# MLP of a decoder block: the second matrix's columns 1024 to 2047 by seven-product blocks too, the residual in HBM meanwhile, another product order and another scheduler

## The chip, the cores and the metric

One core of a Trainium2 chip runs the kernel. The metric is the device time of one execution in microseconds. The median of three runs before the change is 1217.83 us.

Names used below: PE is TensorE (matmuls; PEld its weight loads), DVE is VectorE, ACT is ScalarE, POOL is GpSimd, SP is SyncE, which only issues DMAs here. SBUF is the on-chip memory of 128 partitions, PSUM the eight banks (128 x 512 floats each) into which PE accumulates, HBM the memory outside the core.

## What is computed

One layer of a decoder block on 256 tokens (and 16 meta tokens) of width 2048: two token mixers in parallel, gated and projected, and then an MLP. The change is in the MLP, with small things ahead of it. Cut to what matters:

```python
def reference(...):
    ...
    h = h + rms_norm(m @ w_o[l], g_post_mix[l])
    u = rms_norm(h, g_pre_mlp[l])                         # 256 x 2048
    f = jnp.square(jax.nn.relu(u @ w_up[l])) @ w_down[l]  # 2048 -> 8192 -> 2048
    h = h + rms_norm(f, g_post_mlp[l])
    return h[:, N_META:]
```

All of it is float32. The kernel feeds its matmuls operands cast to the type fp32r, and splits each in two, `hi` (the cast value, made by an ACT copy) and `lo` (the rest, made by a DVE subtraction), and a product of matrices is the sum of three: hi x hi, hi x lo, lo x hi.

## The kernel before

**Stages.** The input projections, the mixers, the gates and the projection by `w_o` come first. From about 544 us on the MLP runs. Its hidden width of 8192 is cut into eight pieces (`NP = 8`) of 1024 features; a piece has two halves h of 512 features, and the 256 tokens have two halves t of 128.

**Up products.** `U{h}{pr}{c}` is a weight block of `w_up`, 1024 rows by 256 columns (half h, pair pr of 128-feature groups, half c of the 2048 rows). It makes hidden features (rows) by tokens (columns) in the PSUM banks u0 and u1, with `mm2_high` (line 418, 512 columns) and `mm2_low` (line 424, 256 columns). After c = 1 the pair of banks is evacuated: `up_pair` adds the two halves of a bank (ACT copy, line 1175; DVE addition, line 1182), and `relu_squared` scales by the row of 1/rms and takes the relu (DVE, line 1201), squares (ACT, line 1206) and writes the activations and their sums and differences ("forms", lines 1217 to 1252) split in hi and lo. That is called an up pair in the prediction. There are eight U blocks and four up pairs in a piece.

**Down products.** A product of a 512 x 512 block of `w_down` with one form of 128 tokens is 12 matmuls of 512 columns (`down`, line 1275). The 2048 output columns are four blocks n of 512. Columns n = 0, 1 are made with a scheme of seven products instead of eight for a 2 x 2 x 2 block (token half, feature half, column block): P1 to P7, each with a weight form made of B11, B12, B21, B22. Two weight forms are made by a DVE addition (`SUM_FOR`, P5 and P6, line 1104), two by a DMA on POOL's queue that adds a block from HBM to a block in SBUF (`BROUGHT_FOR`, P7 and P4, line 1108, "bring"). Each product goes to bank a or b and from there into its block of `F` by a DVE addition (`give`, line 1297). Columns n = 2, 3 are made plainly: X1 to X4, each a weight block used for both token halves, two products each, which stay in the four banks x00, x01, x10, x11 over all pieces. In the last piece all columns are plain (X and Y).

**Weights.** A raw block of 1 MiB comes by a DMA on SP's queue (line 1082) into one of five raw rooms, is split into `hi` (ACT, line 1121) and `lo` (DVE, line 1126), and the raw room is free again. hi and lo have three rooms each (`part_tile`): product m uses room m mod 3, so its split can't begin before product m - 3 has ended on PE.

**Order.** The order of PE's work is written out as text (`FIRST_PIECE`, `PIECE`, `NEXT`, `LAST_PIECE`; a `+` means the next piece). The order of the instructions of the other engines comes from `Plan`: every piece of work has an engine, a cost in us and the buffers it reads and writes; due times are counted back from PE's order, and a list schedule is made with them. In it PE, SP and POOL keep the order in which their work was added (`FIXED`), a DMA costs 3.2 (SP) or 1.0 (POOL) on its engine and is done 2.0 or 9.0 later, and ACT and DVE take among the work that can begin within 0.15 us the one that is due first. The emitted order is fixed; on the chip each engine runs its own list in order and waits where something isn't ready.

**Ends.** At the start of the MLP the squares of h1 (the residual stream, 2 MiB in SBUF, line 1143) give 1/rms, which PE spreads over all partitions (step `R`, `rows2`, line 1164) into `rb`. At the end the row `g_post_mlp` is loaded (line 1395), the sums of squares and the products with g are made per block (line 1414), and `finish_down` (line 1432) adds h1 and writes the result. The last block is made in two halves of 256 columns (`half_done`, lines 1457 to 1463).

Of the kernel before, what the change touches and what calls it, by code (L numbers as in the profile page):

```python
# [14 lines left out]
P = 128  # L15
# [5 lines left out]

class Plan:

    HOP = 0.15
    FIXED = ("PE", "SP", "POOL")
# [24 lines left out]
    def order(self):  # L52
        n = len(self.work)
        after = [[] for _ in range(n)]
        for i, (_, _, _, before, _) in enumerate(self.work):
            for b in before:
                after[b].append(i)
        due, t = [float("inf")] * n, 0.0
        for i, (engine, cost, _, _, _) in enumerate(self.work):
            if engine == "PE":  # L60
                due[i] = t
                t += cost
        for i in reversed(range(n)):
            _, cost, _, _, late = self.work[i]
# [3 lines left out]
        free_at = [0.0] * n  # L68
        clock = {w[0]: 0.0 for w in self.work}
        queue = {e: [i for i in range(n) if self.work[i][0] == e] for e in clock}  # L70
        start = [0.0] * n

        def begin(i):
            return max(clock[self.work[i][0]], free_at[i])
        for _ in range(n):
            best = None
            for e, q in queue.items():
                can = [i for i in (q[:1] if e in self.FIXED else q) if not missing[i]]
                if not can:
                    continue  # L80
                first = min(begin(i) for i in can)
                i = min((i for i in can if begin(i) <= first + self.HOP), key=lambda i: (due[i], i))
                if best is None or begin(i) < begin(best):
                    best = i
            e, cost, _, _, late = self.work[best]
            start[best] = begin(best)
            clock[e] = start[best] + cost
            queue[e].remove(best)
            for a in after[best]:
                free_at[a] = max(free_at[a], clock[e] + late + self.HOP)  # L90
                missing[a] -= 1
# [9 lines left out]
def hybrid_block(ctx: ExitStack, tc: tile.TileContext, ins: dict, out: bass.AP):  # L101
# [30 lines left out]
    psA = ctx.enter_context(tc.tile_pool(name="psA", bufs=6, space=PSUM))  # L132
    psB = ctx.enter_context(tc.tile_pool(name="psB", bufs=2, space=PSUM))
# [220 lines left out]
    u = big.tile([P, KD, 2, -(-L // (4 * LINE)) * 4 * LINE], F32R, tag="um", name="u")[:, :, :, :L]  # L354
# [309 lines left out]
    def block_t(acc, hi, lo, act, kc, nk, t, ks=range(CK)):  # L664
        ts_ = slice(t * P, (t + 1) * P)
        for k in ks:
            kk = kc * CK + k
            for n, (a_, w_) in enumerate(((0, hi), (0, lo), (1, hi))):
                nc.tensor.matmul(acc, act(kk)[:, a_, ts_], w_[:, k, :],  # L669
                                 start=kk == 0 and n == 0, stop=kk == nk - 1 and n == 2)  # L670
# [36 lines left out]
    def u_of(k):  # L707
        return u[:, k, :, M:]
# [64 lines left out]
    def y_of(k):  # L773
        return y[:, k, :, :]
# [28 lines left out]
    def s_act_of(k):  # L803
        return ln["out"][:, k, :, :]
# [73 lines left out]
    def m_of(k):  # L878
        return m[:, k, :, :]
# [131 lines left out]
    F = F_raw[:, :NT * D // 2].rearrange("p (t n c) -> p t n c", t=NT, n=2)  # L1011

# [8 lines left out]

    banks = {"u0": acc_tile("bank_u0"), "u1": acc_tile("bank_u1")}
# [7 lines left out]
    FIRST_PIECE = "U1a0 U1a1 U1b0 R U1b1 P1 X1 X3"  # L1030
    PIECE = "U1a0 U1a1 P1 X1 U1b0 U1b1 X3"
    NEXT = "U0a0+ P5 X2 P6 X4 P7 U0a1+ P3 U0b0+ P2 U0b1+ P4"
    LAST_PIECE = "U1a0 U1a1 Y1 U1b0 U1b1 X1 Y3 Y2 X2 Y4 X3 X4"
    steps = []
    for i in range(NP):
        text = (FIRST_PIECE + " " + NEXT if i == 0 else
                PIECE + " " + NEXT if i < NP - 1 else LAST_PIECE)
# [4 lines left out]
    RAW_OF = {"P1": "B11", "P5": "B11", "P6": "B11", "P4": "B11", "P3": "B22", "P7": "B12",  # L1042
              "P2": "B21"}
    SUM_FOR = {"P5": ("B11", "B12"), "P6": ("B11", "B22")}

    BROUGHT_FOR = {"P7": ("B12", "B22"), "P4": ("B11", "B21")}
    AT = {"B11": (0, 0), "B12": (0, 1), "B21": (1, 0), "B22": (1, 1),
          "Y1": (0, 0), "Y2": (1, 0), "Y3": (0, 1), "Y4": (1, 1),
# [30 lines left out]
    def load(r):  # L1079
        src, (rows, width) = source(*r)  # L1080
        room = room_at[r] = free_rooms.pop(0)
        plan.add("SP", 3.2, lambda: nc.sync.dma_start(
            room_of[room].rearrange("p (k c) -> p k c", k=rows), src),
            writes=(f"raw{room}",), late=2.0)
# [9 lines left out]

    def weights(m_):

        while uses and uses[0][0] <= m_:
# [4 lines left out]
            if what == "sum":  # L1102
                a_, b_ = (room_of[r][:, :CK * CW] for r in rooms)
                plan.add("DVE", 2.29, lambda: nc.vector.tensor_add(a_, a_, b_),
                         reads=names, writes=names[:1])
            elif what[:5] == "bring":
                src, (rows, _) = source(what[6:], raws_[0][1])
                plan.add("POOL", 1.0, lambda: nc.gpsimd.dma_start(
                    room_of[rooms[0]][:, :CK * CW].rearrange("p (k c) -> p k c", k=rows), src,
                    accum_op=ALU.add), reads=names, writes=names, late=9.0)  # L1110
            else:
                box = split_at[m_] = {}
                raw = room_of[rooms[0]][:, :CK * CW]
# [3 lines left out]
                rows, width = HALF if products[m_][0][0] == "U" else (CK, CW)  # L1117

                def high():
# [378 lines left out]
```

## Time and profile before

| | us |
|---|---|
| runs: median (lowest to highest) | 1217.83 (1216.6 to 1218.39) |
| profiled execution, first to last instruction | 1215.2 |
| TensorE busy | 1202.3 |
| VectorE busy | 926.1 |
| ScalarE busy | 616.4 |
| HBM read / written | 248.80 MB / 2.10 MB |

The profiled execution has no separate time of its own on its page beside this span; the runs are timed as a whole, start and end included. A busy time is the sum of an engine's instructions without what overlaps. The granted clock of TensorE is full (0.998 on the mean). In 40 equal slices:

```profile
DVE  5799988999766754587877778778687677786756
DMA  8655555565648656547887767866967867778741
```

Each digit is the busy share of a slice of 30.4 us in tenths; the MLP fills the slices from the 18th on.

### The profile page before, as it was taken

How to read it: one execution, taken by the hardware profiler on the slowest of the kernel's cores; microseconds unless marked ns; L12 is line 12 of the kernel's file. 1: busy time of each engine (PE TensorE's matmuls, PEld its weight loads, DVE VectorE, ACT ScalarE, POOL GpSimd, SP SyncE). 2: the span in 40 equal slices, each digit the busy share in tenths (PEclk: the TensorE clock that was granted, in tenths of full speed). 3: DMA queues.
4: the chain of work that ended last, by engine and by line, in shares of the span. 5: the costliest groups of instructions: out<-in, count | busy, mean ns of one | idle time of the engine just before them, and what ended most of it. 6: DMA issues, size and time to landing. Idle time of an engine off the chain costs nothing.

```text
span 1215.2 us, 15766 instructions
## 1 busy us (share of the span) xinstructions
PE 1202.3 (99%) x6468; PEld 1041.3 (86%) x6468; DVE 926.1 (76%) x1023; ACT 616.4 (51%) x635; POOL 23.7 (2%) x31
## 2 busy tenths in 40 slices
PE   9999999999999999999999999999999999999996
PEld 7999988888888888898888888888888888888885
DVE  5799988999766754587877778778687677786756
ACT  6633335343574344456555565465555555555542
POOL 1000000000000000000000000000000000000000
PEclk9999999999999999999999999999999999999999
DMA  8655555565648656547887767866967867778741
GB/s 255 210 185 184 182 174 196 187 207 177 201 142 274 244 175 203 192 157 227 239 260 208 210 218 210 253 211 189 273 205 204 278 191 227 242 208 238 247 139 70
DMA packets 168872, 251.92 MB, mean 207 GB/s; under 512 B 4209, under 2 KB 91697, under 8 KB 168272
## 3 DMA queue, kind: packets, MB, share of 16 engines
q1 hardware_dynamic: 159632, 230.90, 57.4%
q0 software_dynamic: 8016, 17.98, 7.9%
q10 hardware_dynamic: 1152, 2.04, 0.5%
q8 instruction: 50, 0.82, 0.3%
q14 instruction: 22, 0.18, 0.0%
HBM read 248.80 MB, written 2.10 MB: 206 GB/s over the span
## 4 chain that ended last, share of the span: by engine, by line
PE 97%; DVE 1%; DMA 1%; ACT 0%; ACTq 0%; issue 0%; DVEq 0%
PE bank_u L418 18%; PE acc_gate L669 14%; PE acc_up L1275 14%; PE bank_u L424 9%; PE bank_a L1275 7%; PE acc_o L669 5%; PE bank_b L1275 5%; PE acc_v L413 4%; PE acc_z L413 4%; PE acc_g L413 4%; PE acc_co L669 4%; PE acc_po L669 4%; PE acc_o_last L669 2%; PE acc_up L418 1%; PE bank_u L1275 1%; DMA x_in<-in_x_dram 1%
## 5 line engine op out<-in xcount | busy, mean ns | idle before, releaser
L418 PE MATMUL bank_u<-m,hi 128*128 128x512 f32 x960 | 329.5, 390 | 0.0
L252 ACT CAST hi<-raw 128x2048 fp32r<-128x2048 f32 (+1 forms) x114 | 180.8, 1594 | 228.6 <-PE acc_gate L669 71.5
L255 DVE TENSOR_TENSOR lo<-raw,hi 128x2048 fp32r<-128x2048 f32 (+1 forms) x114 | 215.4, 1895 | 76.1 <-ACT hi L252 75.7
L424 PE MATMUL bank_u<-m,lo 128*128 128x256 f32 x960 | 265.3, 276 | 0.0
L1126 DVE TENSOR_TENSOR lo<-raw_m,hi 128x2048 fp32r<-128x2048 f32 x86 | 196.9, 2290 | 78.4 <-ACT hi L1121 78.3
L1121 ACT CAST hi<-raw_m 128x2048 fp32r<-128x2048 f32 x86 | 164.3, 1911 | 134.5 <-PE bank_u L418 66.4
L418 PEld LDWEIGHTS bank_u<-m,hi 128*128 128x128 f32 x960 | 180.2, 188 | 37.8
L424 PEld LDWEIGHTS bank_u<-m,lo 128*128 128x128 f32 x960 | 180.2, 188 | 1.6
L669 PE MATMUL acc_gate<-hi,u 128*128 128x512 f32 x512 | 158.5, 390 | 0.0
L1275 PE MATMUL acc_up<-hi,forms 128*128 128x512 f32 x496 | 157.6, 389 | 0.0
L479 DVE SCALAR_TENSOR_TENSOR c<-a,taps,c 128x256 f32<-128x256 f32 x240 | 115.4, 483 | 6.6
L669 PEld LDWEIGHTS acc_gate<-hi,u 128*128 128x128 f32 x512 | 96.1, 188 | 19.9
L1275 PEld LDWEIGHTS acc_up<-hi,forms 128*128 128x128 f32 x496 | 93.1, 188 | 19.5
L669 PE MATMUL acc_gate<-lo,u 128*128 128x512 f32 x256 | 99.6, 389 | 0.0
L1275 PE MATMUL acc_up<-lo,forms 128*128 128x512 f32 x248 | 96.6, 389 | 0.0
L1126 DVE TENSOR_TENSOR lo<-raw_c,hi 128x2048 fp32r<-128x2048 f32 x26 | 59.6, 2292 | 37.8 <-ACT hi L1121 37.8
L1126 DVE TENSOR_TENSOR lo<-raw_a,hi 128x2048 fp32r<-128x2048 f32 x31 | 71.0, 2289 | 20.4 <-ACT hi L1121 20.4
L1275 PE MATMUL bank_a<-hi,forms 128*128 128x512 f32 (+1 forms) x256 | 82.0, 383 | 0.0
L1121 ACT CAST hi<-raw_a 128x2048 fp32r<-128x2048 f32 x31 | 59.2, 1911 | 39.9 <-PE bank_u L418 17.1
L1121 ACT CAST hi<-raw_c 128x2048 fp32r<-128x2048 f32 x26 | 49.6, 1907 | 50.4 <-PE bank_u L418 32.3
L1275 PE MATMUL bank_b<-hi,forms 128*128 128x512 f32 (+1 forms) x200 | 63.7, 382 | 0.0
L669 PE MATMUL acc_o<-hi,m 128*128 128x512 f32 x192 | 59.5, 390 | 0.0
(273 smaller groups left out, 1759.1 us busy)
## 6 DMA issues: line engine op xcount, KB each, us to landing
raw<-in_w_in_dram SPq DMA_DIRECT2D x54, 1024.0 KB, 5.1
raw_m<-in_w_down_dram SPq DMA_DIRECT2D x38, 1024.0 KB, 5.5
raw_m<-in_w_up_dram SPq DMA_DIRECT2D x36, 1024.0 KB, 6.0
raw_a<-in_w_up_dram SPq DMA_DIRECT2D x18, 1024.0 KB, 6.1
raw<-in_w_o_dram SPq DMA_DIRECT2D x16, 1024.0 KB, 5.1
raw_c<-in_w_down_dram SPq DMA_DIRECT2D x13, 1024.0 KB, 6.0
raw_a<-in_w_down_dram SPq DMA_DIRECT2D x13, 1024.0 KB, 6.0
raw<-in_w_pool_out_dram SPq DMA_DIRECT2D x8, 1024.0 KB, 5.1
```

The lines of the kernel that those rows point to most:

```text
L252: nc.scalar.copy(hi[:, sl, :], raw[:, sl, :])
L255: nc.vector.tensor_sub(lo[:, sl, :], raw[:, sl, :], f32(hi[:, sl, :]))
L413: nc.tensor.matmul(acc, w[:, k[0], cs], act[:, k[1], a, off:], start=first and n == 0, stop=last and n == 2)
L418: nc.tensor.matmul(acc.rearrange("p (a t) -> p a t", a=2)[:, :, ts], hi[:, k[0], cs], act[:, k[1], :, off + ts.start:off + ts.stop], start ...
L424: nc.tensor.matmul(acc[:, :T], lo[:, k[0], cs], act[:, k[1], 0, off:], start=False, stop=stop, skip_group_check=True)
L479: nc.vector.scalar_tensor_tensor(c, conv["a"][:, q, i:i + T], taps[:, q, i:i + 1], c, op0=ALU.mult, op1=ALU.add)
L669: nc.tensor.matmul(acc, act(kk)[:, a_, ts_], w_[:, k, :], start=kk == 0 and n == 0, stop=kk == nk - 1 and n == 2)
L1121: nc.scalar.copy(box["flat"], raw)
L1126: nc.vector.tensor_sub(lo, raw, f32(box["flat"]))
L1275: nc.tensor.matmul(acc, forms[h][:, f, k, a_, :], box[w_][:, k, cs], start=start and k == 0 and n == 0, stop=stop and k == KH - 1 and n == ...
```

## The change

- Columns n = 2, 3 are made with seven products too, Q1 to Q7 with the weight blocks C11, C12, C21, C22, in pieces 0 to 6. Q2, Q3 and Q4 stay in the banks x00, x10 and x01 over all pieces (`DIRECT`). Q1, Q5, Q6 and Q7 share bank x11 and are added into a new block of totals `G` by `give`; after the last of them `combine` makes the columns' sums out of the four totals with four DVE operations. Q5 and Q6 have a DVE addition for their weights, Q7 and Q4 a bring.
- In the first piece the first addition into a block is an ACT copy with a scale instead of a DVE operation (both for P and for Q).
- `u`, the input of the first stages, is split over two tiles so that the second one's space can hold `G`. The functions that hand out slices of an activation become calls `f(part, tokens)`.
- The second forms tile loses its shift of 16 words.
- h1 is written to HBM (`keep_h1`, a DMA on SP, once the squares are done); its room in SBUF becomes two more raw rooms, seven in all. At the end h1 comes back in two rows into free rooms, after `g_post_mlp`.
- The order of products is another; `R` comes right behind U1a1.
- `Plan.order` is now driven by events: all engines but PE choose the work that is ready and due first, DMAs wait on two queues (SP, POOL), each with one transfer at a time, and the two share the bandwidth. Costs are other numbers.
- In the end stage the banks x00, x01 and x10 are added to `G` (`add_bank`), and the output blocks of columns n = 2, 3 are in `G`.

The last piece stays plain, with the same number of products as before.

```diff
+SUM_FOR = {"P5": ("B11", "B12"), "P6": ("B11", "B22"), "Q5": ("C11", "C12"), "Q6": ("C11", "C22")}
+BROUGHT_FOR = {"P7": ("B12", "B22"), "P4": ("B11", "B21"), "Q7": ("C12", "C22"),
+               "Q4": ("C11", "C21")}
+FIRST_PIECE = "U1a0 U1a1 R U1b0 P1 U1b1 Q1 U0a0+ U0a1+ P5 Q5 Q7 P6 U0b0+ P7 Q6 Q3 P3 P4 Q2 U0b1+ P2 Q4"
+PIECE = "U1a0 Q1 U1a1 U1b0 U1b1 P1 U0a0+ Q5 P5 U0a1+ P6 U0b0+ Q7 Q3 P7 Q6 P3 U0b1+ Q2 P4 P2 Q4"
+LAST_PIECE = "U1a0 U1a1 U1b0 U1b1 X1 X2 Y1 Y3 Y2 Y4 X3 X4"
...
-    HOP = 0.15
-    FIXED = ("PE", "SP", "POOL")
+    HOP = 0.05
+    ISSUE = {"SP": (0.4, 1.0), "POOL": (1.28, 2.2)}
+    LANDS = 1.0
...
+        def begin(e, t):
+            if not idle[e] or not ready[e]:
+                return
+            if e == "PE":
+                if row[0] not in ready[e]:
+                    return
+                i = row.pop(0)
+            else:
+                i = min(ready[e], key=lambda i: (due[i], i))
...
-    u = big.tile([P, KD, 2, -(-L // (4 * LINE)) * 4 * LINE], F32R, tag="um", name="u")[:, :, :, :L]
+    PITCH = -(-L // (4 * LINE)) * 4 * LINE
+    K_FIRST = 13
...
+    u = Tokens((K_FIRST, "um", 0), (KD - K_FIRST, "um8", 3 * LINE))
...
-        room = big.tile([P, b * LINE + KD * T], F32R, tag=f"s{b}", name=f"forms_{b}")
-        forms.append(room[:, b * LINE:].rearrange("p (f k a t) -> p f k a t", f=4, k=KH, a=2))
+        room = big.tile([P, KD * T], F32R, tag=f"s{b}", name=f"forms_{b}")
+        forms.append(room.rearrange("p (f k a t) -> p f k a t", f=4, k=KH, a=2))
...
+    G = big.tile([P, NT, 2, CW], F32, tag="um8", name="G")
...
+    kept = dram.tile([P, NT, D], F32, name="kept")
+    H_ROOMS = (5, 6)
...
-    FIRST_PIECE = "U1a0 U1a1 U1b0 R U1b1 P1 X1 X3"
-    PIECE = "U1a0 U1a1 P1 X1 U1b0 U1b1 X3"
-    NEXT = "U0a0+ P5 X2 P6 X4 P7 U0a1+ P3 U0b0+ P2 U0b1+ P4"
-    LAST_PIECE = "U1a0 U1a1 Y1 U1b0 U1b1 X1 Y3 Y2 X2 Y4 X3 X4"
...
+    def keep_h1():
+        nc.sync.dma_start(kept, h1)
+        room = big.tile([P, len(H_ROOMS), CK * CW], F32, tag="k8", bufs=2, name="raw_h1")
+        for n, r in enumerate(H_ROOMS):
+            room_of[r] = room[:, n, :]
...
-                plan.add("ACT", 1.91, high, reads=names, writes=(f"hi{q}",))
-                plan.add("DVE", 2.29, low, reads=names + [f"hi{q}"], writes=(f"lo{q}",))
+                plan.add("ACT", 1.82, high, reads=names, writes=(f"hi{q}",), late=0.13)
+                plan.add("DVE", 2.22, low, reads=names + [f"hi{q}"], writes=(f"lo{q}",), late=0.13)
...
+            "Q1": "x11", "Q5": "x11", "Q6": "x11", "Q7": "x11",
+            "Q2": "x00", "Q3": "x10", "Q4": "x01"}
+    OPENS = ("P1", "P5", "P2", "Q1", "Q5", "Q6", "Q7")
+    DIRECT = ("Q2", "Q3", "Q4")
...
+        if i == 0 and first_:
+            plan.add("ACT", 0.5, lambda: nc.scalar.activation(dst, bank, AF.Copy, scale=float(sign)),
+                     reads=(BANK[s], name), writes=(name,), late=0.1)
+        else:
+            op = nc.vector.tensor_add if sign > 0 else nc.vector.tensor_sub
+            plan.add("DVE", 0.61, lambda: op(dst, dst, bank), reads=(BANK[s], name),
+                     writes=(name,), late=0.1)
+
+    def combine():
+
+        g1, g6, g7, g5 = (G[:, t, n, :] for t in range(2) for n in range(2))
+
+        def item(op, dst, a_, b_, writes):
+            plan.add("DVE", 0.61, lambda: op(dst, a_, b_), reads=[f"G{k}" for k in range(4)],
+                     writes=(writes,), late=0.1)
+        item(nc.vector.tensor_add, g6, g6, g1, "G1")
+        item(nc.vector.tensor_add, g7, g7, g6, "G2")
+        item(nc.vector.tensor_sub, g6, g5, g6, "G1")
+        item(nc.vector.tensor_sub, g5, g5, g7, "G3")
...
+    def add_bank(t, n, name):
+        dst, blk = total_of(t, n)
+        plan.add("DVE", 0.61, lambda: nc.vector.tensor_add(dst, dst, banks[name]),
+                 reads=(name, blk), writes=(blk,), late=0.1)
...
+    plan.add("SP", 6.0, keep_h1, reads=("ssq2",), writes=[f"raw{r}" for r in H_ROOMS])
+    free_rooms += H_ROOMS
+    loads()
...
+    room_g, *rooms_h = (free_rooms.pop(0) for _ in range(NT + 1))
+    bring_row(room_g, ins["g_post_mlp"].broadcast_to([P, D]))
+    for t, room in enumerate(rooms_h):
+        bring_row(room, kept[:, t, :])
...
+    add_bank(0, NB - 1, "x10")
     sum_of_squares(0, NB - 1)
```

More of the change, by code (lines that the diff above doesn't have):

```diff
@@ L1 @@
+import heapq
+import itertools
 from contextlib import ExitStack
@@ L67, in order @@
         missing = [len(w[3]) for w in self.work]
[L68 to L70 removed]
+        row = [i for i in range(n) if self.work[i][0] == "PE"]
+        ready = {w[0]: [] for w in self.work}
+        idle = dict.fromkeys(ready, True)
         start = [0.0] * n
[L73 to L79, printed above, removed]
[L80 to L91 removed]
```

273 lines of the change are left out of this document (171 added, 102 removed), and 1 row of the table AT.

## The prediction

> **What bounds the kernel now.** I read the engine totals and the chain of waits first, then what TensorE (PE) waits for, then the stages.
>
> ```profile
> span 1215.2 us, 15766 instructions
> PE 1202.3 (99%) x6468; PEld 1041.3 (86%) x6468; DVE 926.1 (76%) x1023; ACT 616.4 (51%) x635; POOL 23.7 (2%) x31
> ...
> PE 97%; DVE 1%; DMA 1%; ACT 0%; ACTq 0%; issue 0%; DVEq 0%
> ```
> ```profile
> PE idle L346 <- POOL ident masks.py:199: 1.4, 1, 1.4
> PE xt L360 <- DMA x_in<-in_x_dram: 1.2, 2, 0.7
> PE acc_grp L413 <- DVE y L732: 0.4, 1, 0.4
> ```
> ```profile
> 620.00:705.00 85.00, 85.00 (x441) 72.72 (x440) 65.29 (x58) 46.01 (x41) 2.55 (x2) 1.00 0.75 225
> 705.00:790.00 85.00, 85.00 (x441) 72.74 (x440) 65.20 (x58) 46.01 (x41) 2.55 (x2) 1.00 0.75 225
> 790.00:875.00 85.00, 85.00 (x441) 72.73 (x440) 65.02 (x57) 46.13 (x42) 2.56 (x2) 1.00 0.75 225
> 1180.00:1215.00 35.00, 25.34 (x135) 21.79 (x133) 23.77 (x43) 10.11 (x22) 0.00 (x0) 0.93 0.16 60
> ```
> ```profile
> 629.56 2.74 PE bank_a L1275 x12
> ...
> 714.12 2.74 PE bank_a L1275 x12
> ...
> 798.68 2.74 PE bank_a L1275 x12
> ```
>
> PE sets the end: it makes 97% of the chain, and its only waits in the whole run are 3.0 us, none of them in the MLP stage, where the windows from 620 to 875 show it busy for all of 85.00 us. In the windows the columns after the length are busy us of PE, PEld, DVE, ACT and POOL, the granted clock, the DMA share and GB/s. The same product (P4, 12 matmuls into bank a) recurs at 629.56, 714.12 and 798.68, so one piece of 1024 hidden features lasts 84.56 us and is nothing but matmuls. One product of 12 matmuls takes 2.74 us; a piece is 8 U products of two such units and 15 single ones, 31 units of 2.73. VectorE (DVE) is busy 65.2 of 85 us there, ScalarE (ACT) 46.0, the DMA engines 0.75 of the time. So a product left out is worth its full 2.74 us as long as nothing else takes PE's place. The last window holds the tail, 35 us with PE busy 25.34.
>
> **The change, part by part.**
>
> *PE.* In 7 pieces X1 to X4, eight products, become Q1 to Q7, seven: 7 x 2.74 = 19.2 us less. Without a wait a piece lasts 84.56 - 2.74 = 81.82 us.
>
> *VectorE.* Each seven-product set needs its own splits, sums and additions.
>
> ```profile
> L1126 DVE TENSOR_TENSOR lo<-raw_m,hi 128x2048 fp32r<-128x2048 f32 x86 | 196.9, 2290 | 78.4 <-ACT hi L1121 78.3
> L1121 ACT CAST hi<-raw_m 128x2048 fp32r<-128x2048 f32 x86 | 164.3, 1911 | 134.5 <-PE bank_u L418 66.4 <-PE acc_up L1275 26.3 <-PE bank_a L1275 11.1
> L1297 DVE TENSOR_TENSOR F_raw<-F_raw,bank_a 128x512 f32<-128x512 f32 x25 | 17.0, 681 | 0.0
> L1104 DVE TENSOR_TENSOR raw_c<-raw_c,raw_m 128x2048 f32<-128x2048 f32 x5 | 11.5, 2291 | 1.5 <-DMA raw_m<-in_w_down_dram 1.5
> ...
> L712 ACT ACTIVATE sg<-acc_gate,r_in 128x512 f32<-128x512 f32 x16 | 10.2, 682 | 0.0
> ```
> ```profile
> 592.72 0.75 DVE L1224 SCALAR_TENSOR_TENSOR F_raw<-F_raw 128x256 f32<-128x256 f32 x2
> 593.39 2.28 DVE L1126 TENSOR_TENSOR lo<-raw_a,hi 128x2048 fp32r<-128x2048 f32 x1
> 595.59 0.68 DVE L1252 TENSOR_TENSOR forms<-F_raw,forms 128x512 fp32r<-128x512 f32 x1
> 596.20 0.75 DVE L1227 TENSOR_TENSOR F_raw<-F_raw 128x256 f32<-128x256 f32 x2
> ```
>
> In the second view (start, duration) the low of 2.28 us starting at 593.39 is followed at 595.59: back to back a 2048-wide operation occupies VectorE 2.20 us, and a 512-wide one (595.59 to 596.20) 0.61. Per piece the change adds 3 splits (seven weights for four) and 2 sums (Q5, Q6), 5 x 2.20 = 11.0, and four additions of a bank into SBUF (Q1, Q5, Q6, Q7; Q2, Q3, Q4 stay in their banks over all pieces), 4 x 0.61 = 2.4: 13.4 us. The window's 65.2 us hold 58 instructions in 85 us; one period of 84.56 has 64.9. VectorE then has 78.3 us in 81.82, 96% against 77%. The spans end some 0.09 us after the next could start, so some 2 us of the 78.3 aren't real where it runs back to back. ACT gets 3 highs of 1.91, 46.0 + 5.7 = 52 us, 63%: no bound. This is the term that can turn the sum, because a low can't be done early: hi and lo have three rooms each, so the split of product m starts when product m-3 ends and must be ready when m-1 ends. With short products that is 2 x 2.74 = 5.48 us for 1.91 + 2.29 = 4.20, a slack of 1.28. The piece's short products are crowded: from P6 to P3, 21.9 us of PE, VectorE owes 7 lows (15.4), two sums (4.4), five additions (3.1) and an up pair (a quarter of what the window's 65.2 leave after 19 lows, 2 sums and 7 additions: 3.7), 26.6 us. The 4.7 too many have to be done ahead, in the 43.8 us from U1a0 to U0a1, where it owes 10 lows, two sums, four additions and two pairs, 36.2 us. It fits, with 2.9 to spare. An addition of 0.61 that gets ahead of a low stays within the slack; a sum of 2.20 doesn't, by 0.92. There are four sums in a piece. I take one of four to come at the wrong moment: 0.9 us a piece, 5.4 in the six pieces after the first. The ends are 0 and 3.7 a piece. I stay near the low end since the sums wait for no part room and two of them can be done in the three U products from U1a1 on (16.4 us).
>
> *DMA.*
>
> ```profile
> GB/s 301 401 65 230 357 361 48 346 124 0 55 299 139 202 355 396 41 13 146 216 264 377 403 69 20 245 233 15 148 207 252 379 401 376 196 206 367 336 105 322
> ...
> q1 hardware_dynamic: 12643, 16.98, 59.9%
> q0 software_dynamic: 1056, 2.10, 15.0%
> ...
> raw_c<-in_w_down_dram POOLq DMA_DIRECT2D x1, 1024.0 KB, 9.6
> ```
> ```profile
> 655.43 1.28 POOL L1108 DMA_DIRECT2D raw_m<-in_w_down_dram  x1 [61.04 <-DVE raw_c L1104]
> ```
>
> In the window 705 to 790 the SP queue's packets took 59.9% of 85 us, 50.9 us for 16.98 MB: 3.14 us of all 16 engines for one load of 1.05 MB. The POOL queue's took 15.0%, 12.75 us for two accumulating loads ("brings"): 6.38 each, landing 9.6 us after issue. The change leaves the 16 loads of a piece (four C weights for X's four) and adds two brings: 50.2 + 25.5 = 75.7 us in 81.82, 93% against 0.75 now. Per piece that is still under PE's time, and the room for it grows from five raw rooms to seven; I take no wait from it in the sum and make its loss a rival. POOL's issue is 1.28 us a bring with up to 61 us of idle time ahead of it; behind a bring that waits for its sum only the next bring is queued, and behind that the split of P7 or Q7, Q4 or P4. The Trainium skill, page "DMA: Bandwidth & Descriptors", section "Anatomy of one DMA — SWDGE (gpsimd) path", gives the movement of data as bytes over 436 GB/s, by which a load would be an estimated 2.4 us and the DMA engines 64 us of 81.8 busy, 78%; the best slices of this window reach 403 GB/s and its mean per load is 3.14 us, so the row decides and the rival below stays.
>
> *Residual in HBM.* One 2.1 MB write on SP's queue, behind the squares of h1, priced as two loads, 6.3 us; every load behind it on SP moves back by that. It falls into the first piece.
>
> ```profile
> 539.88 7.36 SPq L1082 DMA_DIRECT2D raw_m<-in_w_down_dram  x3
> 552.57 0.37 SPq L1082 DMA_DIRECT2D raw_a<-in_w_up_dram  x1
> 557.05 0.37 SPq L1082 DMA_DIRECT2D raw_c<-in_w_down_dram  x1
> 567.93 6.19 SPq L1082 DMA_DIRECT2D raw_m<-in_w_down_dram  x2
> ```
>
> Between 547.2 (end of the three issues) and 567.9 SP issues two loads, 6.3 us of transfer in 20 us, so the write fits where the DMA engines are idle: 0 on the path, with 2.7 us, one product's time, as the other end. At the end two more rows of 1.05 MB come back with g_post_mlp.
>
> ```profile
> 1171.49 0.35 SPq L1395 DMA_DIRECT2D raw_c<-in_g_post_mlp_dram  x1
> ```
> ```profile
> 1200.41 0.69 DVE L1414 TENSOR_TENSOR raw_m<-acc_up,raw_c 128x512 f32<-128x512 f32 x1 [2.63 <-ACT ng_offset=None)_3_0_9216 L860]
> ...
> 1205.39 0.41 DVE L1457 TENSOR_TENSOR last<-raw_m,bank_b 128x256 f32<-128x256 f32 x1
> ```
>
> That row is issued at 1171.49, 34 us before VectorE's first use of h1 after 1202; two loads more (6.3 us) are hidden, and cost up to 6.3 if the rooms come free only with the last splits. Behind X3, X4 one more addition (0.61, bank x10 into G) stands ahead of the 1200.41 multiply, in a stretch where VectorE is hardly idle up to the last half at 1205.39: +0.6 (0 to 0.7). combine's four operations (2.4 us) and two more bank additions run in the last piece, where VectorE owes one low of 2.20 for each 5.46 us of PE: nothing, or their 2.4 if they fell behind the last split.
>
> *First piece's order.*
>
> ```profile
> 563.30 0.60 PE L1164 MATMUL bank_b<-diag,ones 128*128 128x128 f32 x4
> ```
> ```profile
> 558.25 0.48 DVE L1159 TENSOR_SCALAR diag<-ident,r 128x128 f32<-128x128 f32 x2
> ...
> 563.95 0.42 DVE L1378 COPY rb<-bank_b 128x256 f32<-128x256 f32 x1 [1.38 <-PE bank_b L1164]
> ...
> 567.82 1.29 DVE L1236 TENSOR_TENSOR forms<-F_raw,forms 128x512 fp32r<-128x512 f32 x2
> ```
>
> R (the row of 1/rms) moves ahead of U1b0, so it could start 5.46 us earlier, at 557.8, but its diagonals are done at 558.7: PE waits 1.0. From rb (563.95) to the last forms (569.1) are 5.2 us, hidden by U1b0's 5.46 as they are by U1b1 now. I take +1.0; 0 to 3. Then Q7 follows Q5 directly on the same bank, x11, whose content ACT must copy first: 0.68 by the L712 row (a 512-wide read of a bank) when ACT is free, 2.6 when a 1.91 high has just begun; every matmul is queued behind it. I take 1.5.
>
> *Cost figures and rooms.* The planner's new costs only change the order in which ACT, DVE, SP and POOL get their instructions. u in two tiles and the forms without their 16-word shift change addresses; matmuls of all forms in the trace agree at 390 ns whatever room they read, so 0, within 0.5 us either way.
>
> *The sum:* -19.2 + 1.0 + 1.5 + 5.4 + 0.6 = -10.7 us. The profiled execution has 1215.2 between its first and last instruction; the runs' median is 1217.83, and I carry the 2.6 between them unchanged: span 1204.5, time 1207.
>
> **The rivals.**
>
> *VectorE takes PE's place (slower).*
>
> ```profile
> DVE lo L1126 <- ACT hi L1121: 104.5, 72, 3.0
> ```
>
> In the six periods from 620 to 1130 VectorE waited 104.5 us for the high of a weight, 17.4 a piece, because the part rooms come free one product at a time; that now lies in idle time. In the new piece 84.56 - 78.3 = 6.3 us of it are enough to undo the gain; above that the change costs time. If half of it stays (8.7), a piece lasts 87.0 at most and, with the 2 us of overlapped span ends taken off, 85.0 to 87.0, middle 86.0: +1.4 x 7 + 3.1 = +13, 1231 us. For it: the short runs above, one queue for all of VectorE's work, and a fixed order that can't react. Against it: waits shrink when the work ahead of them is late anyway.
>
> *Transfers (no gain).* The DMA engines now idle a quarter of the time, 21 us a window, waiting for rooms. 6.1 us of idle are left in 81.82. If 8.5 of the 21 remain, a piece lasts 84.2: -0.4 x 7 + 3.1, about 1218, no change. Against it: a bring has some 20 us between its sum and its split, and two rooms more let loads run ahead.
>
> *All of it hidden.* Only the copy between Q5 and Q7 stays: -19.2 + 0.7, 1199.
>
> **How the numbers follow.** The forecast, 1207, gets 0.58, with 1200 to 1214 as its own range; everything hidden 0.10; transfers 0.14, of which 0.05 just faster, 0.06 the same and 0.03 slower; VectorE as the bound 0.18. A difference under 0.2%, 2.4 us, can't be told from no change here. Faster: 0.58 + 0.10 + 0.05 = 0.73; same 0.06; slower 0.18 + 0.03 = 0.21. The range, 1199 to 1222, leaves out most of the VectorE case and the very best end.
>
> **What would show it.** Right: 84 matmuls fewer (6384); the last product of a piece every 81.8 to 83 us; 28 brings for 14; windows of a steady piece with VectorE near 78 of 82 us, DMA share near 0.92, and PE waits of under 2 us a piece whose releaser is a DVE lo. The first piece: PE waiting for bank x11 between Q5 and Q7. Wrong: PE waits on lo in every short product, a period over 84.6 (VectorE); or lows and sums waiting for DMA landings with PE behind them (transfers); or a piece period under 82 with the time lost at the start or after 1180.

## The result and the profile after

| | before | after |
|---|---|---|
| runs: median (lowest to highest), us | 1217.45 (1216.6 to 1218.39) | 1200.71 (1199.81 to 1201.93) |
| ratio to before, 95% interval | | 0.9863 (0.9849 to 0.9877) |
| profiled execution, us | 1215.2 | 1198.5 |

The change takes 16.7 us off, 1.4%; 1207 was forecast. The page of the changed kernel, engine totals and chain of waits:

```profile
span 1198.5 us, 15727 instructions
PE 1184.1 (99%) x6384; PEld 1026.1 (86%) x6384; DVE 1013.4 (85%) x1084; ACT 661.4 (55%) x664; POOL 41.7 (3%) x45
...
PE 98%; DMA 1%; DVE 1%; ACT 0%; ACTq 0%; issue 0%; DVEq 0%
```

84 matmuls fewer, 61 instructions more on VectorE (DVE), 14 more on POOL, and TensorE (PE) still makes the chain. All that PE waits for in the run (line waited for, total us, times, longest):

```profile
PE idle L413 <- POOL ident masks.py:199: 1.4, 1, 1.4
PE acc_up L1373 <- ACT G L1398: 0.7, 1, 0.7
PE xt L444 <- DMA x_in<-in_x_dram: 0.6, 2, 0.5
PE acc_grp L497 <- DVE y L816: 0.4, 1, 0.4
```

One of these four lies in the MLP stage: 0.7 us, in the first piece. The windows of a steady piece and of the tail, with the columns of the prediction's windows:

```profile
702.00:784.00 82.00, 82.00 (x426) 70.26 (x425) 77.45 (x65) 52.07 (x45) 5.13 (x4) 1.00 0.91 257
...
1165.00:1198.50 33.50, 22.23 (x121) 19.22 (x119) 21.46 (x42) 10.21 (x22) 0.00 (x0) 0.88 0.17 64
```

PE is busy for all of 82.00 us beside a VectorE busy 77.45 of them (94%) and DMA engines at 0.91. The chain (start, duration) has the end of the first piece and the recurring product of the steady ones:

```profile
588.70 2.73 PE acc_up L1373 x12
591.46 0.61 ACT G L1398
592.11 3.01 PE acc_up L1373 x12
...
627.84 2.72 PE acc_up L1373 x12
...
674.22 2.75 PE bank_a L1373 x12
...
756.06 2.74 PE bank_a L1373 x12
...
837.90 2.74 PE bank_a L1373 x12
```

From 674.22 to 756.06 and to 837.90 are 81.84 us each. This is where the 16.7 us come from, mark by mark: the first piece ends at 627.84 + 2.72 = 630.56, where it ended at 629.56 + 2.74 = 632.30 (-1.7); six steady pieces of 81.84 instead of 84.56 (-16.3); the last piece is the same 65.7 us; and the tail behind PE's last matmul is longer (+1.4, below). The sum is -16.7, to rounding.

What VectorE waits for from 620 to 1112, six pieces, where it waited 104.5 us before:

```profile
DVE lo L1199 <- ACT hi L1194: 24.9, 25, 2.7
```

And the DMA queues from 702 to 784 (packets, MB, share of 16 engines):

```profile
q1 hardware_dynamic: 12553, 16.79, 60.0%
q0 software_dynamic: 2112, 4.19, 30.3%
```

16 loads take 60.0% of 82 us, 3.08 each, and four brings 30.3%, 6.21 each: 74.0 us, against 75.7 forecast.

The tail on VectorE (start, duration, line, operation):

```profile
1181.52 0.69 DVE L1445 TENSOR_TENSOR G<-G,acc_up 128x512 f32<-128x512 f32 x1 [1.18 <-PE acc_up L1373]
...
1184.73 0.16 DVE L932 TENSOR_TENSOR r_mlp<-r_mlp,q_mlp 128x1 f32<-128x1 f32 x1
...
1185.94 0.75 DVE L1556 SCALAR_TENSOR_TENSOR F_raw<-F_raw,r_mlp,raw_m 128x512 f32<-128x512 f32 x1
...
1187.27 0.42 DVE L1583 TENSOR_TENSOR last<-G,bank_b 128x256 f32<-128x256 f32 x1 [0.58 <-PE bank_b L1373]
...
1189.47 0.74 DVE L1556 SCALAR_TENSOR_TENSOR F_raw<-F_raw,r_mlp,raw_m 128x512 f32<-128x512 f32 x1
1190.14 1.41 DVE L1556 SCALAR_TENSOR_TENSOR G<-G,r_mlp,raw_m 128x512 f32<-128x512 f32 x2
1191.46 1.41 DVE L1556 SCALAR_TENSOR_TENSOR F_raw<-F_raw,r_mlp,raw_h 128x384 f32<-128x384 f32 x2
1192.79 1.53 DVE L1556 SCALAR_TENSOR_TENSOR G<-G,r_mlp,raw_h 128x512 f32<-128x512 f32 x3
```

The addition of bank x10 into G (L1445, 1181.52) delays the first token half's factor r (L932), which is ready at 1184.89, 2.4 us ahead of the last half bank (L1583, 1187.27). Only one output operation of that token half (L1556, 1185.94) is made in between, with VectorE idle for 0.58 us behind it; three were before (at 1202.27, 1204.07 and 1204.73, ahead of 1205.39). So eight of them are left behind the second factor instead of six, at some 0.66 us each. From the last half's addition to the end of the span were 9.8 us and are 11.2: +1.4.

### The profile page after: what moved, and what is told of

Same layout as the page of the kernel before. It is cut to its first block, busy times and chain, and to the rows that moved or that the text cites. A ratio compares the mean times of both kernels' runs of the same rounds, so it can differ in the third digit from the quotient of the medians.

```text
span 1198.5 us, 15727 instructions
## 1 busy us (share of the span) xinstructions
PE 1184.1 (99%) x6384; PEld 1026.1 (86%) x6384; DVE 1013.4 (85%) x1084; ACT 661.4 (55%) x664; POOL 41.7 (3%) x45
## 4 chain that ended last, share of the span: by engine, by line
PE 98%; DMA 1%; DVE 1%; ACT 0%; ACTq 0%; issue 0%; DVEq 0%
PE bank_u L502 18%; PE acc_gate L753 15%; PE acc_up L1373 13%; PE bank_u L508 9%; PE bank_a L1373 7%; PE bank_b L1373 5%; PE acc_o L753 5%; PE acc_v L497 4%; PE acc_z L497 4%; PE acc_g L497 4%; PE acc_co L753 4%; PE acc_po L753 4%; PE acc_o_last L753 2%; PE acc_up L502 1%; PE bank_u L1373 1%; DMA x_in<-in_x_dram 1%
## 5 line engine op out<-in xcount | busy, mean ns | idle before, releaser
L1199 DVE TENSOR_TENSOR lo<-raw_m,hi 128x2048 fp32r<-128x2048 f32 x71 | 162.4, 2288 | 15.1 <-ACT hi L1194 14.9
L1194 ACT CAST hi<-raw_m 128x2048 fp32r<-128x2048 f32 x71 | 135.8, 1913 | 51.6 <-PE bank_u L502 18.0
L753 PE MATMUL acc_gate<-hi,u_um 128*128 128x512 f32 x512 | 158.6, 390 | 0.0
L1373 PE MATMUL acc_up<-hi,forms 128*128 128x512 f32 x440 | 143.1, 390 | 0.7 <-ACT G L1398 0.7
L1199 DVE TENSOR_TENSOR lo<-raw_h,hi 128x2048 fp32r<-128x2048 f32 x46 | 105.2, 2287 | 12.8 <-ACT hi L1194 12.7
L1194 ACT CAST hi<-raw_h 128x2048 fp32r<-128x2048 f32 x46 | 88.0, 1913 | 50.5 <-PE bank_u L502 32.5
L753 PEld LDWEIGHTS acc_gate<-hi,u_um 128*128 128x128 f32 x512 | 96.1, 188 | 19.9
L753 PE MATMUL acc_gate<-lo,u_um 128*128 128x512 f32 x256 | 99.6, 389 | 0.0
L1194 ACT CAST hi<-raw_a 128x2048 fp32r<-128x2048 f32 x23 | 44.0, 1912 | 34.0 <-PE bank_u L502 25.1
L1199 DVE TENSOR_TENSOR lo<-raw_a,hi 128x2048 fp32r<-128x2048 f32 x23 | 52.6, 2288 | 11.4 <-ACT hi L1194 11.3
```

What stands on the lines that cost most here:

```text
L753: nc.tensor.matmul(acc, act(kk)(a_, ts_), w_[:, k, :], start=kk == 0 and n == 0, stop=kk == nk - 1 and n == 2)
L1194: nc.scalar.copy(box["flat"], raw_in(room))
L1199: nc.vector.tensor_sub(lo, raw_in(room), f32(box["flat"]))
L1373: nc.tensor.matmul(acc, forms[h][:, f, k, a_, :], box[w_][:, k, cs], start=start and k == 0 and n == 0, stop=stop and k == KH - 1 and n == ...
```

## The experiments

The theory held PE to be the bound, with a VectorE and DMA engines that are nearly full but have room as long as the order of the work is right. The first rival says that VectorE's free time isn't usable, the second that transfers are the next bound, the third that one part alone (rooms, order of products, planner) makes the result and the others do nothing. Times are medians of four to ten runs; the kernel before had 1217.14, 1217.39 and 1217.16 us in the three sets (e1 to e4, e5 to e8, e9 to e12), so differences to the changed kernel's 1200.71 of under 1 us say nothing.

**e1: the changed kernel with the planner of before.** The old class `Plan` and its DMA costs; the costs of the work on VectorE and ScalarE (ACT) stay the new ones.

```diff
-    HOP = 0.05
-    ISSUE = {"SP": (0.4, 1.0), "POOL": (1.28, 2.2)}
-    LANDS = 1.0
+    HOP = 0.15
+    FIXED = ("PE", "SP", "POOL")
...
-        plan.add("SP", 3.1 if r[0][0] == "U" else 2.9, lambda: nc.sync.dma_start(
+        plan.add("SP", 3.2, lambda: nc.sync.dma_start(
...
-                plan.add("POOL", 5.9, lambda r=rooms[0], k=rows, src=src: nc.gpsimd.dma_start(
+                plan.add("POOL", 1.0, lambda r=rooms[0], k=rows, src=src: nc.gpsimd.dma_start(
```

> The changed kernel with the planner of before: its rule (PE, SP and POOL in the order in which work was added, 0.15 us per hop) and its DMA costs (3.2 + 2.0 us a load, 1.0 + 9.0 us a bring). Products, product order, seven raw rooms and the DVE and ACT costs stay. Theory A (the new planner is what lets VectorE stand at 95% without PE waiting): PE waits of 1 to 4 us a piece come back, a piece lasts 83 to 86 us instead of 81.84, the time is 1208 to 1230. Theory B (the product order has slack enough by itself, any planner that looks at due times finds it): at most 0.3 us a piece, 1199 to 1203.

Measured: 1235.43 us (1234.08 to 1238.55), 1.0154 of before (1.0139 to 1.017), above theory A's range. PE's main wait, and one of VectorE's from 620 to 1112:

```profile
PE bank_u L446 <- DVE F_raw L1222: 15.9, 6, 3.8
```
```profile
DVE raw_c L1155 <- DMA raw_a<-in_w_down_dram: 4.5, 1, 4.5
```

The same work in another order on ACT, DVE, SP and POOL turns a gain of 16.7 into a loss of 18.3. VectorE stands for 4.5 us at a sum (L1155) whose second block hasn't landed (five such waits, 19.2 us, in the six pieces), and everything behind the sum on VectorE stands too, among it the evacuation of an up pair's banks (L1222) for which PE waits. In the changed kernel no operation of VectorE waits for a landing in these pieces: this planner puts the sum ahead of the time at which its block is there.

**e2: one raw room less.** Six rooms instead of seven; h1 still goes to HBM and back.

```diff
-    H_ROOMS = (5, 6)
+    H_ROOMS = (5,)
```

> The changed kernel with six raw rooms instead of seven; the write of h1 to HBM and its return stay. Theory A (the rooms that the residual's move frees are needed, since C11, B11, C12, B12, B22 and C22 are held together for a while and U blocks need a room beside them): loads start later, DVE lows and sums wait for landings, PE waits 1 to 5 us a piece, 1208 to 1235. Theory B (the DMA engines at 90% are fed well enough with six): within 0.3 us a piece, 1199 to 1203.

Measured: 1235.62 us (1235.15 to 1235.89), 1.0152 (1.0137 to 1.0167), just above theory A's range. PE's longest waits in total, and a step of the chain from 714 to 800:

```profile
PE bank_u L508 <- DVE lo L1199: 12.2, 10, 1.6
PE acc_up L1373 <- DVE lo L1199: 11.8, 8, 1.7
```
```profile
749.02 9.59 DMA raw_m<-in_w_down_dram
```

One room is worth 34.9 us here. Lows become the releaser of PE, and the chain behind them runs through transfers (9.59 us for one); VectorE's sums wait 10.9 us for landings in the six pieces, and none did with seven rooms. The DMA engines aren't fuller there (0.85 to 0.90 in the windows), so it isn't their rate. That leaves the loads' wait for a free room; it follows from the edit, no row measures it by itself. This is the transfer rival's path, and the seventh room closes it.

**e3: the changed kernel with a product order in the pattern of before.**

```diff
-PIECE = "U1a0 Q1 U1a1 U1b0 U1b1 P1 U0a0+ Q5 P5 U0a1+ P6 U0b0+ Q7 Q3 P7 Q6 P3 U0b1+ Q2 P4 P2 Q4"
+PIECE = "U1a0 U1a1 P1 Q1 U1b0 U1b1 U0a0+ P5 Q5 P6 Q6 P7 Q7 U0a1+ P3 Q3 U0b0+ P2 Q2 U0b1+ P4 Q4"
```

> The changed kernel with the steady pieces' products in the order of before, Q's put where the X's stood (U1a0 U1a1 P1 Q1 U1b0 U1b1 U0a0+ P5 Q5 P6 Q6 P7 Q7 U0a1+ P3 Q3 U0b0+ P2 Q2 U0b1+ P4 Q4); planner and rooms are the new ones. Theory A (the new product order is needed: six short products in a row, with four sums and two brings for them, are 16.4 us of PE and some 26 us of VectorE, and a bring lands 9.6 us after its sum): PE waits 5 to 12 us a piece, more than the 2.74 us saved, 1235 to 1275. Theory B (the due-first planner evens it out): under 2 us a piece, below 1215.

Measured: 1226.19 us (1225.31 to 1226.98), 1.0075 (1.0059 to 1.009), between the two theories' ranges. PE's longest wait in total:

```profile
PE bank_b L1373 <- DVE forms L1350: 9.2, 6, 2.1
```

The order matters, 25.5 us, but PE's wait isn't for lows: once a piece a product in bank b waits for a form (L1350), and in five of the six cases a sum (L1211) stands right ahead of that form on VectorE (the sum at 839.18, the form at 841.38). 9.2 us and 2.6 of another form don't make 25.5. The granted clock is a part of the rest: 0.96 in the first window of 82 us from 620 on and 0.98 in the next four, against 1.00 in the changed kernel. That is an estimated 10 us (0.04 and four times 0.02 of 82), good to some 2 us since the clock is given to 0.01 (last section).

**e4: the kernel before with the new planner alone.** Its rule and its costs of DMAs, highs and lows; the other costs stay the old ones.

```diff
-    HOP = 0.15
-    FIXED = ("PE", "SP", "POOL")
+    HOP = 0.05
+    ISSUE = {"SP": (0.4, 1.0), "POOL": (1.28, 2.2)}
+    LANDS = 1.0
```

> The kernel before with nothing changed but the planner (new rule, new costs for DMAs, highs and lows). PE does not wait in the MLP of the kernel before, so both theories expect the same time, 1216 to 1219, within 0.1% of before. A gain of 2 us or more would mean that part of the 16.7 us comes from the planner and not from the seven products left out.

Measured: 1218.2 us (1217.9 to 1219.87, ten runs), 1.0009 (1.0000 to 1.0019). The planner alone gives nothing, since PE waited for nothing in the MLP before. It is a condition of the gain, not a source. e1 to e3 speak against the third rival: planner, room and order are each needed. By itself only the planner was tried. That the room or the order alone would give nothing either is argued, from PE not waiting in the MLP before. The smaller parts (ACT copies in the first piece, R's place, u in two tiles, the forms' shift) were not tried one by one.

**e5, e6, e12: more work for VectorE.** Four, eight and two additions of 512 columns into a scrap tile in each of the six steady pieces, free to run from the piece's first product on.

```diff
+        if s == "U1a0" and 0 < i < NP - 1:
+            for _ in range(4):
+                plan.add("DVE", 0.61, extra, reads=("go",), late=0.1)
```

> The changed kernel with four more VectorE operations of 512 columns (0.61 us each, 2.4 us) in each of the six steady pieces; nothing depends on their result, they only stand in VectorE's queue. VectorE has 77.5 us of work in a piece of 81.84, so 79.9 then. Theory A (VectorE is near its limit, the lows' narrow windows leave hardly more than it has now): PE waits begin, 0.5 to 2.5 us a piece, 1204 to 1216. Theory B (its idle time is usable almost to the end, the planner fills it): under 0.3 us a piece, 1200 to 1203.

> The same with eight operations, 4.9 us: 82.4 us of VectorE's work in 81.84 of PE's. Theory A: VectorE sets the end with its remaining waits on top, 2 to 5 us a piece, 1213 to 1231. Theory B: only what is over, 0.5 to 1 us a piece, 1204 to 1208. No change would mean that VectorE can do more in a piece than its busy time says.

> The changed kernel with two more VectorE operations of 512 columns (1.2 us) in each of the six steady pieces. Four cost 8.7 us and eight 17.2. If VectorE has no slack at all in its narrow stretches: 0.5 to 1 us a piece, 1203 to 1206. If the first 1.2 us fit in its idle time and the loss begins above: 1200 to 1202.

| additions a piece | work, us | median (lowest to highest) | ratio to before (95%) | against 1200.71 |
|---|---|---|---|---|
| 2 (e12) | 1.2 | 1200.02 (1199.74 to 1200.41) | 0.9859 (0.9845 to 0.9872) | -0.7 |
| 4 (e5) | 2.4 | 1209.41 (1209.28 to 1209.63) | 0.9931 (0.9917 to 0.9945) | +8.7 |
| 8 (e6) | 4.9 | 1217.89 (1215.17 to 1222.84) | 1.0005 (0.9993 to 1.0017) | +17.2 |

With 1.2 us more, the window of a steady piece and VectorE's waits (620 to 1112):

```profile
702.00:784.00 82.00, 82.00 (x426) 70.22 (x425) 78.67 (x67) 52.06 (x45) 5.13 (x4) 1.00 0.92 257
```
```profile
DVE lo L1199 <- ACT hi L1194: 17.3, 20, 2.7
```

PE is still busy for 82.00 of 82.00, and VectorE's waits for highs fell from 24.9 to 17.3 us, by 1.3 a piece: the work went into those waits. That is the claim "waits shrink when the work ahead of them is late anyway", measured. With 2.4 us PE waits. Its main wait in e5, and the chain at one of them:

```profile
PE acc_up L1373 <- DVE forms L1350: 7.1, 5, 1.4
```
```profile
828.13 0.89 DVE raw_m L1211
...
830.25 0.70 DVE forms L1350
830.99 2.55 PE acc_up L1373 x10
```

In five of the six pieces a product waits 1.4 us for a form, and 8.7 us in five waits are 1.7 each. What stands ahead of the form on VectorE is a sum (L1211, from 828.05 on), and in the changed kernel the two stand the other way round:

```profile
825.78 0.68 DVE L1350 TENSOR_TENSOR forms<-F_raw,forms 128x512 fp32r<-128x512 f32 x1
826.38 2.28 DVE L1211 TENSOR_TENSOR raw_m<-raw_m,raw_c 128x2048 f32<-128x2048 f32 x1
```

So it is in all five pieces of e5 that wait; in its first steady piece the form comes ahead of the sum, and PE doesn't wait. All six pieces of e6 and, with no work added at all, all six of e9 below have the sum ahead of the form and the same 1.4 us. The step between 1.2 and 2.4 us goes with one exchange in the planner's order, not with VectorE's time running out: e6 has twice the added work of e5, and PE waits only 0.2 us longer a piece. As this planner places the work, between 1.2 and 2.4 of the 82.00 - 77.45 = 4.55 us that VectorE has idle in a piece can be used. How much an order that keeps the form ahead could use was not tried. e6's time, inside theory A's range, has another part, the granted clock (last section).

**e7: Q7 not right behind Q5.** An attempt to take the wait of the first piece away.

```diff
-... P5 Q5 Q7 P6 U0b0+ P7 Q6 ...
+... P5 Q5 P6 Q7 U0b0+ P7 Q6 ...
```

> The changed kernel with Q7 and P6 exchanged in the first piece (P5 Q5 P6 Q7), so that ACT has 2.7 us to copy bank x11. The one PE wait of the MLP, 0.7 us, goes, and with the pipeline's drain about 1.0 us of the time: 1199.7 against 1200.7. If the wait turns up at another place (the bring for Q7, VectorE's sum for P6 earlier), no change.

Measured: 1206.89 us (1205.36 to 1207.6), 0.9907 (0.9892 to 0.9922): 6.2 us slower than the changed kernel instead of 1 faster. PE's new waits, and VectorE's timeline at the place:

```profile
PE bank_a L1373 <- DVE lo L1199: 3.6, 1, 3.6
...
PE bank_a L1373 <- ACT hi L1194: 1.1, 1, 1.1
```
```profile
586.94 2.28 DVE L1211 TENSOR_TENSOR raw_c<-raw_c,raw_m 128x2048 f32<-128x2048 f32 x1
...
592.27 2.28 DVE L1199 TENSOR_TENSOR lo<-raw_a,hi 128x2048 fp32r<-128x2048 f32 x1
594.48 2.29 DVE L1199 TENSOR_TENSOR lo<-raw_c,hi 128x2048 fp32r<-128x2048 f32 x1
```

The wait of 0.7 for the copy is gone and 4.7 us of others stand in its place; PE runs at a lower clock behind them (last section), which is most of the other 2.2 us. P6's weight (raw_c) gets its sum only at 586.94 to 589.22, and then another sum (at 590.07) and Q7's low (raw_a, 592.27) go ahead of P6's low at 594.48, which PE needs first. The order Q5 Q7 P6 is paid with 0.7 us and buys the time for P6's sum.

**e8, e11: seven products for columns 0 and 1 in the last piece too.** e8 has e7's swap beside it, e11 has the first piece as it was and another order.

```diff
-LAST_PIECE = "U1a0 U1a1 U1b0 U1b1 X1 X2 Y1 Y3 Y2 Y4 X3 X4"
+LAST_PIECE = "U1a0 U1a1 U1b0 U1b1 P1 X1 P5 P6 X2 P3 P7 P2 P4 X3 X4"    (e8)
+LAST_PIECE = "U1a0 U1a1 U1b0 U1b1 X1 P2 P1 P5 P6 X2 P7 P3 P4 X3 X4"    (e11)
```

> The exchange of the run before, and in the last piece columns 0 to 1023 by the seven products P1 to P7 as in the other pieces (U1a0 U1a1 U1b0 U1b1 P1 X1 P5 P6 X2 P3 P7 P2 P4 X3 X4); columns 1024 to 2047 of it stay plain. One product less, 2.7 us, for three more splits, two sums, two brings and three more bank additions on VectorE, which idles a third of the last piece. If VectorE's slack there is enough: 1196 to 1197.5. If P's short products crowd it near the end: PE waits of 1 to 4 us on lows or on P7's and P4's brings, 1198 to 1201, nothing gained over the run before.

> The changed kernel's first piece, and in the last piece columns 0 to 1023 by seven products as in the run with the last piece before, now in another order: U1a0 U1a1 U1b0 U1b1 X1 P2 P1 P5 P6 X2 P7 P3 P4 X3 X4, so that P5 comes 10.9 us after U1b1 instead of 8.2 and no two neighbours share a bank. If the waits there came from the order (P5's form not ready): one product less, 2.7 us, 1197.5 to 1199. If VectorE can't carry the last piece's end beside its own sums and products with g: 1200 to 1205, no gain over the changed kernel.

Measured: e8 1212.78 us (1210.96 to 1214.2), 0.9958 (0.9945 to 0.9971); e11 1211.36 (1210.21 to 1211.56), 0.995 (0.9937 to 0.9962). Both miss: the product left out, 2.74 us, costs 5.9 in e8 (against e7's 1206.89) and 10.7 in e11 (against 1200.71). The two longest of PE's new waits in e11:

```profile
PE bank_b L1371 <- ACT forms L1332: 3.1, 1, 3.1
PE bank_a L1371 <- DVE lo L1199: 2.2, 1, 2.2
```

In the last piece no U products of a next piece stand between the seven, so forms (L1332, L1334), sums and brought blocks come due within a few short products. With a high (1.1) and another form (0.8) the new waits are 7.2 us of the 13.4 that are lost beside the product (10.7 + 2.74); a granted clock of 0.94 from 1112 to 1165 and 0.86 from there to 1187, 1.00 in the changed kernel, is an estimated 6 us more (0.06 of 53 and 0.14 of 22). The waits are shown; that no order avoids them is not. So no version here beats the changed kernel (e12's 1200.02 is that kernel with idle work in it, the same within the spread).

**e9, e10: the new planner's rule with one half of its old numbers.** e9 takes back the costs on PE, ACT and DVE, their delays `late` and `HOP`; e10 only the transfers.

```diff
-                plan.add("DVE", 2.22, low, reads=names + [f"hi{q}"], writes=(f"lo{q}",), late=0.13)    (e9)
+                plan.add("DVE", 2.29, low, reads=names + [f"hi{q}"], writes=(f"lo{q}",))
...
-        plan.add("ACT", 0.53, square, reads=(s_name,), writes=(s_name,), late=0.1)
+        plan.add("ACT", 0.75, square, reads=(s_name,), writes=(s_name,))
...
-    ISSUE = {"SP": (0.4, 1.0), "POOL": (1.28, 2.2)}    (e10)
+    ISSUE = {}
```

> The changed kernel with the new planner's rule and its DMA model, but the costs of before for VectorE, ScalarE and PE (2.29 a low, 1.91 a high, 0.69 an addition, 0.42 for a 256-wide operation and so on, no separate latency, 0.15 us a hop). By those costs VectorE's work of a piece is a few us more than the measured one, so that in the plan VectorE is the bound and the order drifts from what the chip does. If the measured costs are what the old planner lacked: PE waits 2 to 5 us a piece, 1212 to 1235. If the rule matters and the costs don't: 1199 to 1204.

> The changed kernel with the new rule and the new costs of VectorE, ScalarE and PE, but the DMA model of before: a load holds SP for 3.2 us and lands 2.0 later, a bring holds POOL for 1.0 and lands 9.0 later, and the two do not slow each other. If the shared bandwidth of the two queues is what the plan has to know (the DMA engines are 90% busy): landings come later than planned, VectorE waits for them in front of other work, PE waits 1 to 5 us a piece, 1206 to 1235. If seven rooms let loads run far enough ahead: 1199 to 1203.

Measured: e9 1212.13 us (1211.81 to 1213.06), 0.996 (0.9944 to 0.9975); e10 1210.16 (1209.11 to 1210.66), 0.9941 (0.9927 to 0.9954). PE's main wait in e9 and in e10:

```profile
PE acc_up L1371 <- DVE forms L1348: 8.5, 6, 1.4
```
```profile
PE bank_u L502 <- DVE F_raw L1278: 5.5, 6, 1.3
```

Planner costs that are off by 0.07 in 2.22 us for a low, 0.08 in 0.61 for an addition and 0.22 in 0.53 for a square, without the delay `late` behind them and with 0.15 instead of 0.05 us a hop, cost 11.4 us on the chip; which of these does it was not tried. The wait is the one of e5: the sum (830.59) stands ahead of the form (832.79). Transfers that are counted as a fixed time each, without slowing each other, cost 9.5, and VectorE's sums wait 8.4 us for landings in the six pieces of e10. If the parts of e1's 34.7 add up, the other 25 us are the old rule with its longer hop; no run has that alone.

## Why the prediction was right, and where its size was off

**PE stays the bound; seven products out of the path.** Right: -19.2 was forecast, and each steady piece is 2.72 us shorter, with nothing given back. The signs that it named came too: 6384 matmuls, a period of 81.84, VectorE 77.45 of 82, the DMA engines at 0.91, PE's wait for bank x11. Only the waits on a low didn't.

**"I take one of four to come at the wrong moment: 0.9 us a piece, 5.4 in the six pieces after the first."** This term was mis-sized: it measured 0, its low end, and it is most of the 6.3 us between forecast and result. The mechanism exists: in e3, e5, e6 and e9 one sum a piece stands ahead of a form that PE needs, at 1.7 us each where the clock stays up (1.4 of wait and 0.3 behind it), and it is a form that comes late, not a low. The working priced a low's slack of 1.28 us against a sum of 2.20 and took the sum's moment as if left to chance. The planner sets it, with costs near the measured ones, and in the changed kernel no sum comes at the wrong moment. With other costs (e9) the term would have been real, and larger than forecast.

**VectorE's load.** Forecast 78.3 us of 81.82 by the rows, "some 2 us" of it not real; measured 77.45 in 82.00. Its waits for highs, 17.4 us a piece before, fell to 4.2 (24.9 over six). Of its "2.9 to spare" in a piece between 1.2 and 2.4 could be used in this planner's order (e12, e5).

**Transfers.** Forecast 75.7 us a piece, measured 74.0; no PE wait from them, as taken in the sum. e2 shows that this holds by one room.

**Residual, 0.** As taken: in the tail no operation of VectorE waits for a row of h1. The "34 us" between the load of g_post_mlp and the first use are 31 by the numbers beside it (1171.49 to 1202); nothing hung on it.

**R, +1.0.** Mis-sized, 0. The reason given, diagonals done at 558.7, carried a time over from the old order. In the new one they are made earlier:

```profile
554.38 0.48 DVE L1255 TENSOR_SCALAR diag<-ident,r 128x128 f32<-128x128 f32 x2
```
```profile
557.86 0.60 PE L1260 MATMUL bank_b<-diag,ones 128*128 128x128 f32 x4
```

VectorE has them done by 554.86, and PE's four matmuls (L1260) follow the last of U1a1 at 557.86 without a wait.

**Q5 to Q7, 1.5.** The place and the releaser were right (the only PE wait of the stage). The size was near its low end: ACT was free, the copy took 0.61 us (591.46), the wait 0.7, and the next product 3.01 us instead of 2.72: 1.0 in all.

**The tail, +0.6.** The added bank addition is where it was said to be, but the tail grew by 1.4. The working counted the 0.61 us itself, not that a factor later by it leaves two more output blocks behind the last half.

The terms by their measures: -19.0 (7 x 2.72) + 0 (R) + 1.0 (Q5 to Q7) + 0 (VectorE) + 1.4 (tail) = -16.6, where -16.7 was measured. The three small terms, 3.1 in the forecast, came to 2.4; that this is so near is luck, since R is 1.0 too high, Q5 to Q7 0.5 too high and the tail 0.8 too low.

**The rivals.** "All of it hidden", 1199, came nearest, at a chance of 0.10. VectorE in PE's place, 1231, didn't happen. e1's 1235.43 comes near that case, though there VectorE also stands waiting for transfers. What spoke for it, "a fixed order that can't react", holds. The prediction passed over what decides: of the new costs it said that they "only change the order in which ACT, DVE, SP and POOL get their instructions", and on a VectorE at 94% that order is worth 9 to 35 us (e10, e9, e1).

## What to carry to other kernels

When one engine sets the time and the next is at 94%, its idle time isn't spare time as a matter of course: price it by how long the next operation can be late, measure it by adding idle work until the bound engine waits, and then look at what changed places, since here one exchange made the step. A static order made by a planner is as good as its costs; here costs off by 0.07 to 0.22 us for most operations, with no delays and a longer hop, took back 11.4 of 16.7 us, so take costs from back-to-back starts in a trace and model queues that share bandwidth. A part of a change that gives nothing by itself (here the planner, e4) may still be what the gain needs (e1). Taking out one part at a time from the complete version shows that; adding it to the old version does not.

## What the runs showed of the hardware

**A wait can cost more than its length, by the granted clock.** e5 and e6 have the same PE wait of 1.4 us for the same form, once a piece. In e5 the clock stays at 1.00, and ten matmuls behind it take 2.55 us (above). In e6, the windows and the chain at that place:

```profile
832.00:836.00 4.00, 2.58 (x8) 1.84 (x8) 4.00 (x4) 1.22 (x1) 0.00 (x0) 0.76 0.01 4
836.00:840.00 4.00, 4.00 (x16) 3.24 (x15) 3.10 (x7) 2.81 (x3) 0.00 (x0) 0.81 0.78 246
```
```profile
833.63 4.14 PE acc_up L1373 x10
```

The granted clock is 0.76 and 0.81 in two windows of 4 us, and ten matmuls take 4.14 us: 1.6 us more than in e5. Three of e6's six windows of 82 us show 0.98 and three 1.00. The traces narrow it down. Behind the wait of 1.4 alone, in e5's five cases and e9's six, the clock never drops. Where PE also stood idle for 0.14 to 0.20 us some 0.7 us earlier, in five pieces each of e6 and e3, it drops in seven of ten (in e6's sixth that gap is 0.08, and it doesn't); in e3 ten matmuls take 4.15 us at 842.12 and only 2.56 at 1098.79, behind the same two gaps. What decides between those stays open. e6's runs differ with it: from the shortest, 1215.17 us, to the longest, 1222.84, the granted clock of the run goes from 0.996 to 0.989. In e7, behind waits of 4.7 us, it lasts longer:

```profile
596.00:600.00 4.00, 3.18 (x8) 2.51 (x9) 4.00 (x5) 0.00 (x0) 1.28 (x1) 0.50 0.91 273
600.00:604.00 4.00, 4.00 (x16) 3.23 (x15) 1.45 (x3) 2.29 (x2) 0.00 (x0) 0.84 1.07 197
```

The Trainium skill, page "TensorE: Matmul & The Clock Gate", section "Part 1: The HAM clock gate (the "warmup" mystery)", tells of a clock that is halved after at least one idle window of about 3.4 us, in windows that run free of the kernel. e7, with a single wait of 3.6, agrees with it; in e6 no wait of the MLP is longer than 1.4, and the clock drops all the same.

**The product behind a wait is longer.** 3.01 us at 592.11 in the changed kernel, where its neighbours take 2.72, and in e5 2.55 us for ten matmuls that take 2.27 at that rate: some 0.3 on top of the wait, which is why 1.4 us of wait cost 1.7 in e5.
